# Moving the start address of the weight tiles by 192 bytes within 512

## The chip, the core and the metric

The kernel runs on one core of one Trainium2 chip. The metric is the device time of one execution in microseconds (us). Times of single instructions are in nanoseconds (ns).

## The reference, cut to what matters

The reference runs two networks of two layers each, one after the other, on 256 tokens of 1024 features in float32. The first (below "block 1") has three attention branches and a feed-forward product of width 4096 per layer. The second ("block 2") has gated feed-forward products of width 2816, a retention layer, and a neighbourhood attention. Almost all arithmetic is dense products of this kind:

```python
proj = h @ w_in[layer]
h_res = h_res + merged @ w_out[layer]
h_res = h_res + jnp.square(jax.nn.relu(h2 @ w_ff1[layer])) @ w_ff2[layer]
...
def swiglu(x, w_in, w_out):
    a, b = jnp.split(x @ w_in, 2, axis=-1)
    return (jax.nn.silu(a) * b) @ w_out
```

## The kernel before, in words

Features lie on the 128 partitions, tokens along the free dimension. A float32 product is made of three products of float32r parts: each operand is split into a rounded high part and the rest, and `mm3` (L393 to L397) adds high times high (L395), low weight times high input (L396) and high weight times low input (L397). One such matmul loads a stationary tile of 128 x 128 and streams a moving tile past it. In `mmw` (the dense products) the stationary operand is a chunk of 128 weight columns and the moving operand the activations. In `token_major` (value products of block 2) it is the other way round: activations stand and 256 weight columns move.

`load_w` (L376) fetches a weight block of up to 128 x 1024 into a `raw` tile (ring of four), ScalarE copies it to `whi` (L386, the high part), and VectorE writes the rest to `wlo` (L387). Both `whi` and `wlo` are rings of four tiles of 4096 bytes per partition. All three come from the pool `wp`, in which tags are laid out one after another in the order of first use: `raw`, `whi`, `wlo`. Pools stand behind one another in memory, so that what is added to `wp` moves everything that was opened after it.

The moving operand is 272 columns wide in most of block 1 (256 tokens and 16 others; 256 in parts of it, above all in layer 1), and 512 or 256 in block 2 (two streams of 256 tokens together, or one).

Adding up the tiles' sizes in this order gives the byte address of each tile within a partition. Modulo 512 the program of before has:

```
tile                                              start modulo 512
raw, whi, wlo (every ring buffer, every 128-column chunk)     128
block 1: hh0, hl0, hh1, hl1, ...   64, 128, 192, 256, ... (tiles of 1088 bytes)
block 1, layer 0: uh0, ul0, uh1, ... (moving, 272 wide)   192, 256, 320, ...
block 1, layer 1: uh, ul (moving, 256 wide)                     0
block 2: hh, hl, uh, ul, ra, rb, noh, nol (moving)            320
block 2, retention: ra, rb, pth, ptl (stationary), rvh, rvl (moving)   320
```

A chunk of 128 float32 columns is 512 bytes, so each chunk of a weight tile has the start of its tile. In the retention layer some products take no weights: `scores` multiplies `ra`/`rb` tiles with each other, and `outputs` takes `pth`/`ptl` as stationary and `rvh`/`rvl` as moving operand. Both go through the same `mm3` as the dense products, and in both the two operands start at 320.

The order of the work is the program's order on each engine; the framework puts semaphores between writers and readers. Nothing in this order depends on addresses.

Of the kernel before, what the change touches and what calls it, by code (L numbers as in the profile page):

```python
# [34 lines left out]
# ---------------------------------------------------------------- host layout  # L35
def blocks(w, n):
    """[K, N] -> [N/n, 128, (K/128)*n], contiguous per block and partition."""
    k, m = w.shape
    return np.ascontiguousarray(
        w.reshape(k // P, P, m // n, n).transpose(2, 1, 0, 3)  # L40
    ).reshape(m // n, P, (k // P) * n)


def wide(w):
    """[1024, N] -> [N/256, 2, 128, 4*256]: blocks of 256 columns, in two halves of rows."""
    return np.ascontiguousarray(np.stack([blocks(w[:512], 256), blocks(w[512:], 256)], axis=1))


def cols(v):
    """[n*128] -> [128, n]."""  # L50
    return np.ascontiguousarray(v.reshape(-1, P).T)


def rep(v):
    """vector -> the same vector in each of the 128 partitions."""
    return np.ascontiguousarray(np.broadcast_to(v.reshape(1, -1), (P, v.size)))
# [8 lines left out]
def feat(x):  # L65
    """[tok, 1024] -> [128, 8, tok]."""
    return np.ascontiguousarray(x.T.reshape(KC, P, -1).transpose(1, 0, 2))


# order of a 64-wide rotary head in which partners lie 16 partitions apart  # L70
# [65 lines left out]
def nat_bias(rpb):  # L136
    """[16, 15, 31] -> [16, 128, 2, 256]; outside the windows the fill value."""
    h = rpb.shape[0]
    src = np.concatenate([rpb.reshape(h, 15 * 31), np.full((h, 1), NEG, rpb.dtype)], axis=1)
    q = np.arange(T)  # L140
    r, c = q[:, None] // 64, q[:, None] % 64
    a, cc = q[None, :] // 64, q[None, :] % 64
    start = np.clip(c - 8, 0, 48)
    inside = (cc >= start) & (cc < start + 16)
    idx = np.where(inside, (a - r + 7) * 31 + np.clip(cc - c + 15, 0, 30), 15 * 31)
    b = np.take(src, idx.reshape(-1), axis=1).reshape(h, 2, P, T)
    return np.ascontiguousarray(b.transpose(0, 2, 1, 3)).reshape(h, P, 2 * T)
# [80 lines left out]
# ------------------------------------------------------------------- the chip  # L228
def body(tc, a, off, outs, stop=None):
# [34 lines left out]
    # ---- residual, constants, small vectors  # L264
# [34 lines left out]
    # ---- modulations: silu(c) and silu(c_ctx), in every partition, times the rows of w_mod^T  # L299
# [39 lines left out]
    def decays():  # L339
        # log sigmoid of the decays: min(x, 0) - 2 atanh(e / (2 + e)), e = exp(-|x|)  # L340
        dec = V("dec")
        e, den, s2, po = (tl(mini, [P, 8], f"lg{i}", bufs=1) for i in range(4))
        act.activation(e, dec, AF.Abs)
        act.activation(e, e, AF.Exp, scale=-1.0)
        dve.tensor_scalar(den, e, 2.0, None, op0=ALU.add)
        dve.reciprocal(den, den)
        dve.tensor_tensor(e, e, den, ALU.mult)
        dve.tensor_tensor(s2, e, e, ALU.mult)
        dve.tensor_scalar(po, s2, 1.0 / 17, 1.0 / 15, op0=ALU.mult, op1=ALU.add)
        for d in (13, 11, 9, 7, 5, 3, 1):  # L350
            dve.tensor_tensor(po, po, s2, ALU.mult)
            dve.tensor_scalar(po, po, 1.0 / d, None, op0=ALU.add)
        dve.tensor_tensor(po, po, e, ALU.mult)
        dve.tensor_scalar(lg, dec, 0.0, None, op0=ALU.min)
        dve.scalar_tensor_tensor(lg, po, -2.0, lg, ALU.mult, ALU.add)
        dve.tensor_scalar(nlg, lg, -1.0, None, op0=ALU.mult)
        dve.tensor_scalar(lg256, lg, 256.0, None, op0=ALU.mult)
# [13 lines left out]
    def finish(l, j):  # L371
        """the modulations of layer l up to its part j."""
        while len(todo) > (DEPTH - l) * 72 - 24 * (j + 1):
            step()

    # ---- weights: raw, and its two float32r parts  # L376
    def load_w(src):
        done[0] += 1
        if done[1] and done[0] % done[1] == 0:
            step()  # L380
        n = src.shape[-1]
        raw = tl(wpool, [P, 1024], "raw", bufs=RAW)
        nc.sync.dma_start(raw[:, :n], src)
        hi = tl(wpool, [P, 1024], "whi", F32R, bufs=4)
        lo = tl(wpool, [P, 1024], "wlo", F32R, bufs=4)
        act.activation(hi[:, :n], raw[:, :n], AF.Copy)  # L386
        dve.tensor_tensor(lo[:, :n], raw[:, :n], hi[:, :n].bitcast(F32), ALU.subtract)  # L387
        return hi, lo
# [4 lines left out]
    def mm3(out, w, x, start, stop):  # L393
        """out += w^T x of the parts (hi, lo) of both."""
        pe.matmul(out, w[0], x[0], start=start, stop=False)  # L395
        pe.matmul(out, w[1], x[0], start=False, stop=False)  # L396
        pe.matmul(out, w[0], x[1], start=False, stop=stop)  # L397

    def mmw(out, w, xs, base=0, stride=P, first=True, last=True):
        """out = sum over chunks k of W[:, k]^T x_k, W[:, k] at base + k*stride."""  # L400
        m = len(xs)
        for k, x_ in enumerate(xs):
            o = base + k * stride
            mm3(out, cut(w, slice(o, o + P)), x_, first and k == 0, last and k == m - 1)

    def lead(ws, xs, parts):
        """the first products after a norm, in the order in which its outcome appears."""
# [8 lines left out]
    # ---- dense products in between the steps of the attentions  # L416
    queue, late = [], []

    def fill():
        """the next dense products of the queue, then what waits for the earlier ones."""  # L420
        d = late[:]
        late.clear()
        if queue:
            queue.pop(0)()
        for f in d:
            f()
# [4 lines left out]
    def weave(gens, lag):  # L431
        """runs the generators, a new one every lag rounds, with dense products in between."""
# [14 lines left out]
    def rstd(ss, n, N):  # L447
        """(ss / n + eps) ** -0.5, as float32."""
# [11 lines left out]
    class Sq:  # L460
        """sums of squares over the features, gathered while the residual grows; the last
        chunk comes in parts of the columns."""
# [18 lines left out]
        def end(self, i, *xs):  # L481
            """the last chunks of part i; the very last one meets the others in the product."""
# [26 lines left out]
    # ================================================================ block 1  # L509
    # The products of a norm take x * gain; what they give is scaled by the rstd of the tokens.  # L510
    class Grown:
        """x[:, c0:] times a gain, as parts, and the sums of squares, chunk by chunk."""
# [31 lines left out]
    def block1_layer(l, grown):  # L544
# [23 lines left out]
        def sq2_of(p, N):  # L568
            """the squares, in their two parts."""
# [12 lines left out]
        # ---- latent projections of the first branch  # L582
        def scaled(p, t, r):
            """the products of a norm, scaled by the rstd of the tokens."""
            dve.tensor_tensor(t, p, r, ALU.mult)
            return t
# [21 lines left out]
        def rope(p, N, g, cos, sin, dst):  # L608
            """dst = rotary(p * g), partners 16 partitions apart."""
# [13 lines left out]
        # ---- softmax attention, query-major scores  # L623
# [6 lines left out]
        def qscale(s, om, m, n, scale):  # L630
            """scale * rsqrt of the mean squares of the queries: [128, segs, m] (queries on partitions)."""
# [16 lines left out]
        def probs(S, qsc):  # L648
            """exp(s - max) [128, SW] of the scaled scores, and 1 / sum [128, segs]."""
# [13 lines left out]
        def transposed(e):  # L663
            """[keys, queries]: latent key tiles [128, 384], first keys [16, Q]."""
# [15 lines left out]
        def attend(heads, v):  # L680
            """heads: (out rows, first value column, width, transposed probabilities)."""
# [74 lines left out]
        # ---- dense products that run between the steps of the attentions  # L756
# [28 lines left out]
        # gates and branch projections, merged in the tiles of the first gates  # L785
# [45 lines left out]
        # ---- stick-breaking attention, key-major scores  # L831
# [46 lines left out]
        # ---- differential attention  # L878
# [75 lines left out]
        def close(k, p, c0, dst, grown):  # L954
            """x_k += p, and what the next norm takes of it."""
# [10 lines left out]
        # ---- feed forward  # L966
# [39 lines left out]
    # ================================================================ block 2  # L1006
# [13 lines left out]
    def ada(l, j, sq, vs):  # L1020
        """the modulated norm of the streams vs, in the parts of sq."""
# [14 lines left out]
    def grow(l, j, vs, prod, sq=None):  # L1036
        """x_k += gate * products, with the squares of it; the last two chunks stream by stream."""
# [21 lines left out]
    def ffn(l, s, j, sq, vs, nparts, every=2):  # L1059
        """one gated feed forward over the streams vs."""  # L1060
# [33 lines left out]
    def token_major(w, h, t, p):  # L1094
        """p = tokens t of h times a block of 256 columns, given in two halves of rows."""
# [4 lines left out]
    def retention(sq):  # L1100
# [8 lines left out]
        def decay(hd):  # L1109
            lf, nlb = lg[:, hd:hd + 1], nlg[:, 4 + hd:5 + hd]  # L1110
            # decays between the streams (first half) and within one (second half)
# [58 lines left out]
        def scores(cd, qk):  # L1170
            # scores, key-major, times the decays
# [78 lines left out]
    def nat(sq):  # L1250
# [30 lines left out]
        def unit(h2, qt):  # L1281
            """one pair of heads over one tile of queries."""
# [63 lines left out]
    class Start:  # L1346
        """the sums of squares of the context, and then of the other stream."""
# [57 lines left out]
```

## Time and profile before

| | |
|---|---|
| median of three runs | 2953.26 us (2950.34 to 2953.97) |
| span of the profiled execution, first to last instruction | 2944.5 us, 8.8 us under the median |
| busy: TensorE / weight loads / VectorE / ScalarE / GpSimd | 99% / 87% / 67% / 48% / 8% |
| mean DMA rate | 144 GB/s |

The profiled execution has no time of its own beside its span; the 8.8 us are what the device time has around it, as far as one execution tells.

TensorE is busy from end to end, but a busy share doesn't tell how fast it goes: the ends of matmuls are modelled and overlap the next. The rate is read from the starts of consecutive matmuls. In what follows, the interval is the time from one matmul's start to the next, taken from the first and last start of a stretch and the number of steps between them.

### The profile page before, as it was taken

The numbers are of one execution on the slowest core, as the hardware profiler recorded it, in microseconds if no ns is written. First come the engines' busy times: TensorE is split into PE (matmuls) and PEld (weight loads), VectorE is DVE, ScalarE is ACT, GpSimd is POOL, SyncE is SP. The second block draws the span as 40 slices with busy tenths as digits, with TensorE's granted clock in tenths as the row PEclk, the third lists the DMA queues.
The fourth block names the chain that finished last, engine by engine and source line by source line (L and its number), as shares of the span: only waits on it lengthen the run. The fifth ranks groups of instructions, "written<-read, shape, count | busy, mean of one in ns | idle before, by whom it ended". The sixth has DMA issues, their size and how long they took to land.

```text
span 2944.5 us, 46123 instructions
## 1 busy us (share of the span) xinstructions
PE 2907.9 (99%) x18084; PEld 2556.6 (87%) x18084; DVE 1975.5 (67%) x3370; ACT 1405.4 (48%) x2487; POOL 241.3 (8%) x216
## 2 busy tenths in 40 slices
PE   8999999999999999999999999999999999999998
PEld 8899999989899988888888888888888888877998
DVE  8787876878876665565776767656566565555665
ACT  7767554677665432334433435332343223444554
POOL 2121100212201000001110101000010000100000
PEclk9999999999999999999999999999999999999999
DMA  6344666545467544442343332444334444332464
GB/s 205 115 131 137 193 199 202 163 136 158 147 209 226 177 144 137 142 147 93 122 134 122 109 115 93 143 143 144 128 108 145 137 141 130 102 108 90 157 188 143
DMA packets 122906, 424.46 MB, mean 144 GB/s; under 512 B 13632, under 2 KB 20160, under 8 KB 122560
## 3 DMA queue, kind: packets, MB, share of 16 engines
q1 hardware_dynamic: 121248, 419.50, 45.2%
q8 instruction: 143, 2.34, 0.3%
q10 hardware_dynamic: 1440, 2.00, 0.2%
q14 instruction: 75, 0.61, 0.1%
HBM read 420.40 MB, written 1.05 MB: 143 GB/s over the span
## 4 chain that ended last, share of the span: by engine, by line
PE 92%; DVE 4%; ACT 2%; issue 1%; DMA 0%; POOL 0%; DVEq 0%; ACTq 0%; POOLq 0%
PE acc L395 28%; PE acc L397 28%; PE acc L396 28%; DVE wlo L387 1%; ACT whi L386 1%; PE att L645 1%; PE att L395 1%; PE att L396 1%; PE att L397 1%; PE att L843 1%; PE acc L1317 0%; PE nr L1307 0%; DVE xn L1030 0%; PE att L1287 0%; DVE hl L1032 0%
## 5 line engine op out<-in xcount | busy, mean ns | idle before, releaser
L386 ACT ACTIVATE whi<-raw 128x1024 fp32r<-128x1024 f32 (+2 forms) x650 | 677.8, 1044 | 828.6 <-PE acc L397 774.2
L395 PE MATMUL acc<-hh,whi 128*128 128x512 f32 (+2 forms) x3200 | 1060.6, 332 | 11.6 <-ACT hh L521 6.2
L396 PE MATMUL acc<-hh,wlo 128*128 128x512 f32 (+2 forms) x3200 | 1053.9, 330 | 2.9 <-DVE wlo L387 2.9
L397 PE MATMUL acc<-hl,whi 128*128 128x512 f32 (+2 forms) x3200 | 1053.4, 331 | 0.3 <-DVE hl L1032 0.3
L387 DVE TENSOR_TENSOR wlo<-raw,whi 128x1024 fp32r<-128x1024 f32 (+2 forms) x650 | 789.0, 1215 | 348.2 <-ACT whi L386 314.7
L395 PEld LDWEIGHTS acc<-hh,whi 128*128 128x128 f32 x3200 | 604.8, 189 | 81.7 <-ACT hh L521 6.2
L396 PEld LDWEIGHTS acc<-hh,wlo 128*128 128x128 f32 x3200 | 604.0, 189 | 63.0 <-DVE wlo L387 3.6
L397 PEld LDWEIGHTS acc<-hl,whi 128*128 128x128 f32 x3200 | 601.7, 188 | 61.2 <-DVE hl L1032 0.9
L326 DVE SCALAR_TENSOR_TENSOR dump<-raw,cs 128x1024 bf16<-128x1024 f32 x288 | 354.7, 1231 | 230.2 <-DMA raw<-in_wmod_dram 228.0
L397 PE MATMUL acc<-ul,whi 128*128 128x256 f32 (+2 forms) x1258 | 410.9, 327 | 0.4
L395 PE MATMUL acc<-uh,whi 128*128 128x256 f32 (+2 forms) x1258 | 410.7, 327 | 0.0
L396 PE MATMUL acc<-uh,wlo 128*128 128x256 f32 (+2 forms) x1258 | 409.8, 326 | 0.0
L397 PEld LDWEIGHTS acc<-ul,whi 128*128 128x128 f32 x1258 | 236.4, 188 | 23.0 <-DVE ul L445 1.0
L395 PEld LDWEIGHTS acc<-uh,whi 128*128 128x128 f32 x1258 | 236.9, 188 | 22.3
L396 PEld LDWEIGHTS acc<-uh,wlo 128*128 128x128 f32 x1258 | 236.7, 188 | 22.3
L479 POOL TENSOR_TENSOR sqacc<-sqacc,sq 128x256 f32<-128x256 f32 (+2 forms) x60 | 75.6, 1260 | 1889.0 <-ACT sq L474 1888.6
L456 ACT ACTIVATE sig<-acc 128x512 f32<-128x512 f32 (+1 forms) x88 | 48.1, 546 | 279.8 <-PE acc L397 279.8
L1042 DVE SCALAR_TENSOR_TENSOR x<-acc,gmod,x 128x256 f32<-128x256 f32 x136 | 65.7, 483 | 172.0 <-PE acc L397 171.3
L395 PE MATMUL acc<-whi,hh 128*128 128x256 f32 x384 | 108.0, 281 | 0.2 <-ACT nq L1261 0.2
L397 PE MATMUL acc<-wlo,hh 128*128 128x256 f32 x384 | 107.6, 281 | 0.0
L396 PE MATMUL acc<-whi,hl 128*128 128x256 f32 x384 | 107.3, 279 | 0.0
L1081 DVE TENSOR_TENSOR sig<-acc,sig 128x512 f32<-128x512 f32 (+1 forms) x88 | 54.9, 624 | 59.7 <-PE acc L397 56.8
(319 smaller groups left out, 3523.2 us busy)
## 6 DMA issues: line engine op xcount, KB each, us to landing
raw<-in_fin_dram SPq DMA_DIRECT2D x176, 512.0 KB, 3.7
raw<-in_wmod_dram SPq DMA_DIRECT2D x144, 512.0 KB, 3.6
raw<-in_wf_dram SPq DMA_DIRECT2D x128, 512.0 KB, 4.1
raw<-in_win_dram SPq DMA_DIRECT2D x104, 512.0 KB, 3.7
raw<-in_fout_dram SPq DMA_DIRECT2D x64, 448.0 KB, 3.4
raw<-in_fout_dram SPq DMA_DIRECT2D x32, 512.0 KB, 4.2
raw<-in_rin_dram SPq DMA_DIRECT2D x32, 512.0 KB, 3.5
raw<-in_wbr_dram SPq DMA_DIRECT2D x24, 512.0 KB, 3.6
```

What stands on the lines that cost most here:

```text
L326: dve.scalar_tensor_tensor(dump, raw, 1.0, cs[:, v], ALU.mult, ALU.mult, accum_out=m[:, v, b:b + 1])
L386: act.activation(hi[:, :n], raw[:, :n], AF.Copy)
L387: dve.tensor_tensor(lo[:, :n], raw[:, :n], hi[:, :n].bitcast(F32), ALU.subtract)
L395: pe.matmul(out, w[0], x[0], start=start, stop=False)
L396: pe.matmul(out, w[1], x[0], start=False, stop=False)
L397: pe.matmul(out, w[0], x[1], start=False, stop=stop)
L456: act.activation(dst, src, AF.Exp, scale=-1.0, **k)
L479: eng.tensor_tensor(self.acc[:, :N], self.acc[:, :N], s[:, :N], ALU.add)
L645: pe.matmul(S[:, c:c + n], q[rows, t0 - q0:t0 - q0 + P], k[rows, 0:n], start=False, stop=i == ns - 1)
L843: pe.matmul(Z[:m, c + lo - k0:c + n], sbk[h2][rows, k0:k0 + m], sbq[h2][rows, lo - q0:Q], start=False, stop=k0 == 0)
L1042: dve.scalar_tensor_tensor(d, p[:, i * T:i * T + T], G(l, vs[i], j, k), d, ALU.mult, ALU.add)
L1081: dve.tensor_tensor(g, pb, g, ALU.mult)
```

## The change

Two tiles that nothing reads or writes are added to the pool `wp`: `gap` (48 floats, 192 bytes) before the first `whi` tile, and `gap1` (80 floats, 320 bytes) behind the first use of `wlo`. So `whi` and `wlo` start at 320 instead of 128 modulo 512. `raw` stays where it was. Both gaps together are 512 bytes, so every tile laid out behind the rings moves by 512 and keeps its start modulo 512. The rest of the diff replaces comments and docstrings by empty lines; it is not shown. With the six new lines, L386 and L387 become L392 and L393, and L395 to L397 become L401 to L403.

```diff
+    gap = []
+
     def load_w(src):
...
         raw = tl(wpool, [P, 1024], "raw", bufs=RAW)
         nc.sync.dma_start(raw[:, :n], src)
+        if not gap:
+            gap.append(tl(wpool, [P, 48], "gap"))
         hi = tl(wpool, [P, 1024], "whi", F32R, bufs=4)
         lo = tl(wpool, [P, 1024], "wlo", F32R, bufs=4)
+        if len(gap) == 1:
+            gap.append(tl(wpool, [P, 80], "gap1"))
         act.activation(hi[:, :n], raw[:, :n], AF.Copy)
```

## Rows read from the trace of the kernel before

**Rows 1.** The page: busy time by engine, granted clock in 40 slices, end-setting chain.

```profile
PE 2907.9 (99%) x18084; PEld 2556.6 (87%) x18084; DVE 1975.5 (67%) x3370; ACT 1405.4 (48%) x2487; POOL 241.3 (8%) x216
...
PEclk9999999999999999999999999999999999999999
...
PE 92%; DVE 4%; ACT 2%; issue 1%; DMA 0%; POOL 0%; DVEq 0%; ACTq 0%; POOLq 0%
```

**Rows 2.** TensorE's groups by shape, 1012 to 2945 us: count, busy us, mean ns.

```profile
L395 PE MATMUL acc<-hh,whi 128*128 128x512 f32 x1312 | 519.0, 396 | 0.3 <-DVE sig L1080 0.3
...
L395 PE MATMUL acc<-uh,whi 128*128 128x512 f32 x486 | 192.2, 396 | 0.0
...
L395 PE MATMUL acc<-hh,whi 128*128 128x256 f32 x540 | 151.9, 283 | 4.0 <-ACT hh L1031 2.4 <-DVE sig L1080 1.7
...
L395 PE MATMUL acc<-whi,hh 128*128 128x256 f32 x384 | 108.0, 281 | 0.2 <-ACT nq L1261 0.2
...
L395 PE MATMUL acc<-uh,whi 128*128 128x256 f32 x260 | 73.1, 281 | 0.0
...
L397 PE MATMUL acc<-rb,whi 128*128 128x512 f32 x120 | 47.4, 396 | 0.0
```

**Rows 3.** Timeline, 512-wide dense products: start us, duration us, engine, line.

```profile
1500.21 0.39 PE L395 MATMUL acc<-hh,whi 128*128 128x512 f32 x1
1500.22 0.19 PEld L396 LDWEIGHTS acc<-hh,wlo 128*128 128x128 f32 x1
...
1511.41 0.39 PE L395 MATMUL acc<-hh,whi 128*128 128x512 f32 x1
```

**Rows 4.** Timeline, retention's `outputs`, 512 wide, no weights.

```profile
1443.79 0.39 PE L395 MATMUL att<-rvh,pth 128*128 128x512 f32 x1
...
1444.49 1.05 ACT L386 ACTIVATE whi<-raw 128x1024 fp32r<-128x1024 f32 x1
...
1444.94 0.39 PE L397 MATMUL att<-rvl,pth 128*128 128x512 f32 x1
...
1451.74 0.39 PE L397 MATMUL att<-rvl,pth 128*128 128x512 f32 x1
```

**Rows 5.** Timeline, retention's `scores`, 512 wide, behind a pause of TensorE.

```profile
1431.43 0.40 PE L396 MATMUL att<-ra,rb 128*128 128x512 f32 x1
...
1432.60 0.39 PE L395 MATMUL acc<-hh,whi 128*128 128x512 f32 x1
```

**Rows 6.** Timeline, 256-wide dense products of the last feed-forward.

```profile
2800.81 0.28 PE L395 MATMUL acc<-uh,whi 128*128 128x256 f32 x1
...
2805.91 0.28 PE L395 MATMUL acc<-uh,whi 128*128 128x256 f32 x1
```

**Rows 7.** Timeline, retention's `scores`, 256 wide, no weights.

```profile
1428.27 0.28 PE L396 MATMUL att<-ra,rb 128*128 128x256 f32 x1
...
1429.47 0.28 PE L397 MATMUL att<-rb,ra 128*128 128x256 f32 x1
```

**Rows 8.** Timeline, `token_major` products, weights moving.

```profile
1525.10 0.28 PE L395 MATMUL acc<-whi,hh 128*128 128x256 f32 x1
...
1530.76 0.28 PE L395 MATMUL acc<-whi,hh 128*128 128x256 f32 x1
```

**Rows 9.** Timeline, second feed-forward product of block 1, layer 1.

```profile
949.92 0.28 PE L395 MATMUL acc<-uh,whi 128*128 128x256 f32 x1
...
955.98 0.28 PE L395 MATMUL acc<-uh,whi 128*128 128x256 f32 x1
```

**Rows 10.** Timeline, second feed-forward product of block 1, layer 0, 272 wide.

```profile
479.80 0.29 PE L395 MATMUL acc<-uh,whi 128*128 128x272 f32 x1
...
485.83 0.29 PE L395 MATMUL acc<-uh,whi 128*128 128x272 f32 x1
```

**Rows 11.** TensorE's groups by shape, 0 to 1012 us.

```profile
L395 PE MATMUL acc<-hh,whi 128*128 128x272 f32 x816 | 239.0, 293 | 6.2 <-ACT hh L521 6.2
...
...
L395 PE MATMUL acc<-uh,whi 128*128 128x256 f32 x256 | 72.0, 281 | 0.0
```

## The prediction

> **What bounds the kernel.** I read four views. First the page [rows 1]: TensorE is busy 99% of the span, 92% of the chain that ends last is its matmuls, and the granted clock is full in every slice, so the upper of its two levels (2.4 GHz) holds throughout. TensorE therefore sets the time, and what matters is how fast its stream of matmuls runs, not who waits. Second, its groups by shape, for the counts [rows 2, 11]. Third, the timeline inside long stretches, for the interval between starts. At 2.4 GHz one column per cycle would be 213.3 ns for 512 columns (512/2.4) and 106.7 ns for 256. The 512-wide dense products don't reach this: 48 steps from 1500.21 to 1511.41 us are 11.20 us, 233.3 ns each, 20 ns or 48 cycles over 512 [rows 3]. Beside each running matmul the next stationary tile is loaded, starting within 0.01 us of it [rows 3]. So two reads of SBUF run side by side, and 9% of the stream is something other than columns.
>
> Fourth, I looked for matmuls of the same shape whose two operands stand otherwise modulo 512. Retention's `outputs` is that: 512 wide, the same `mm3`, the same clock, moving at 320 as in the dense products, but the stationary tile at 320 and not at 128. Its first five steps take 1.15 us (230 ns each), and then 30 steps from 1444.94 to 1451.74 us take 6.80 us: 226.7 ns, 32 cycles over 512 [rows 4]. ScalarE writes a `whi` tile in the middle of this without disturbing it. This is where the change would put all weights. At 256 columns the comparison turns round: the dense products (moving 320, stationary 128) step at 113.3 ns (45 steps, 5.10 us) [rows 6], and `scores`, with both at 320, at 120.0 ns (10 steps, 1.20 us) [rows 7]. These are 16 and 32 cycles over 256. So the relative start is worth 16 cycles a matmul, a gain at 512 columns and a loss at 256.
>
> **The change part by part.** The two gap tiles have no instruction: no DMA, no wait, no semaphore. What stands behind the rings moves by 512 bytes and keeps its start modulo 512. What is left is the new start of `whi` and `wlo` against the other operand. I take it that the start modulo 512 of the two operands decides, and price each class by the row with the same pair of starts.
>
> 1. 512-wide dense products, block 2, moving 320, stationary from 128 to 320. Count 3 x (1312 + 486 + 120) = 5754 [rows 2]. From 233.3 to 226.7 ns: 5754 x -6.67 = -38.4 us. Settling costs 5 steps of 230 instead of 226.7 ns, 17 ns each time [rows 4]. Only where the stream is broken must it settle anew; I allow 60 times, an estimate, +1 us. The other bound is that it never settles: the five steps behind a pause take 1.17 us, 234 ns [rows 5], a change of +4 us. I take the settled value, because rows 4 show 30 steps of it against 5 of the other.
> 2. 256-wide dense products, block 2, moving 320, stationary from 128 to 320. Count 3 x (540 + 260) = 2400 [rows 2], and by the code 192 in the neighbourhood layer's last product and 48 in retention's last: 2640. From 113.3 to 120.0 ns: +17.6 us. The other bound is that they stay at 113.3, 0 us. I take 120, the only row with this pair.
> 3. `token_major`, 3 x 384 = 1152 [rows 2], moving from 128 to 320, stationary at 320. Now 5.66 us for 48 steps, 117.9 ns [rows 8]; after it the pair is that of rows 7, 120.0 ns: +2.4 us. Bounds 113.3 and 120: -5.3 to +2.4 us.
> 4. Block 1, layer 1, second feed-forward product: moving 0, stationary from 128 to 320, 3 x 256 = 768 [rows 11]. Now 6.06 us for 51 steps, 118.8 ns [rows 9]. After it the stationary tile stands 320 ahead of the moving one, and in rows 6 it stands 320 ahead modulo 512 too (128 - 320 = -192, which is 320). So I take 113.3 ns: -4.2 us. Bounds 113.3 and 120: -4.2 to +0.9 us.
> 5. The rest of block 1. Moving tiles are 1088 bytes, so from tile to tile the start steps by 64, and over eight tiles every multiple of 64 is met. Shifting the weights by 192 mostly permutes the pairs: 0 us. The largest classes, 272 wide, count 3 x 816 in the first products [rows 11] and by the code 768 in the second of layer 0, together 3216; they take 125.6 ns a step (6.03 us for 48) [rows 10]. The bounds scale rows 6 and 7 by 272/256: 120.4 and 127.5 ns, so 3216 x -5.2 = -16.7 to 3216 x +1.9 = +6.1 us. An average over eight starts stays far from either.
> 6. ScalarE's copy to `whi` and VectorE's difference meet new starts too. ScalarE is busy 48% and VectorE 67% of the span [rows 1], under TensorE's stream. Were each of the 650 weight blocks 0.1 us dearer on both, the 130 us more would still go into idle time; only where TensorE is waiting for a block, 1% of the span, could some show.
>
> The sum is -38.4 + 1 + 17.6 + 2.4 - 4.2 = -21.6 us. It is made against the profiled execution's span of 2944.5 us, which it takes to 2922.9. The 8.8 us between that span and the median of 2953.3 us lie outside the stream and stay, so the forecast is 2931.7 us, 0.7% less. It passes to the end almost in full, since the stream is the chain; where DVE or ACT stands in the chain (6%) no dense product is being cut.
>
> The trace shows a loading weight and a running matmul that cost each other 16 to 48 cycles a step, by their starts [rows 3, 4, 6, 7]. The Trainium skill says otherwise: its page "TensorE: Matmul & The Clock Gate" (Part 2, step by step) gives TensorE two independent read ports, so that loading the next weights takes no bandwidth from the running matmul, and "SBUF — State Buffer" (Who interferes with whom) has it that "PE and ACT never wait on anyone". By that rule the sum would be 0 and the time 2953.3 us; the rows speak against it here.
>
> **The rivals.**
>
> A. *The start does not decide; nothing moves.* The fast 512-wide rows would then owe their 226.7 ns to something else in `outputs`: another PSUM ring (`att`, not `acc`), or both operands being activations. For it: all of rows 4 and 7 come from one layer. Against it: the same layer shows 226.7 at 512 columns and 120.0 at 256, which no general advantage explains, and the PSUM ring is the same in both. Time 2953 us, within 0.2%, which is about what a measurement of this kernel can tell from no change. The rule of the Trainium skill's page "TensorE: Matmul & The Clock Gate" (Part 2), named above, ends here too; no row shows it.
>
> B. *The 512-wide products don't settle; slower.* There is more than one steady step for one pair of starts: rows 5 show 234 ns with the pair that rows 4 show at 226.7. If the dense products of block 2, with their waits for weights at the head of a group, stay in the slow one, the losses of classes 2 to 4 stand alone: 4 + 17.6 + 2.4 - 4.2 = +20 us, 2973 us. It turns from gain to loss where the mean 512-wide step is above 233.3 - (17.6 + 2.4 - 4.2)/5754 = 230.6 ns, so where 59% of the stream is at 233.3. Against it: the five steps at 234 are all there is of it.
>
> C. *The 256-wide products keep their step.* If a steady step of 113.3 ns exists for the new pair too, classes 2 and 3 cost nothing or gain: -38.4 + 1 - 5.3 - 4.2 = -46.9 us, 2906 us. For it: more than one steady step for a pair is possible, as rows 4 and 5 say. Against it: ten equal steps of 120.0 in rows 7.
>
> **How the numbers follow.** The forecast has 0.73, A 0.11, B 0.08, C 0.08. The predicted time is the forecast's, 2931.7 us. Its own range: class 1 down to three quarters of its gain (+10), class 5 between half its lower bound and all of its upper (-8 to +6), class 2 a third less (-6): 2918 to 2947 us. All of it is faster by over 0.2%. With A the cases hold 0.84; so the range reaches from 2918 to A at 2955 and leaves out B and C. Faster 0.73 + 0.08 = 0.81, within 0.2% 0.11, slower 0.08.
>
> **What would show it.** In the profile after, at the same clock: 512-wide dense steps of 226.7 ns and not 233.3 in the feed-forwards of block 2; 256-wide steps of 120.0 and not 113.3 in the last feed-forward, whose 1584 matmuls (by the code, 44 x 24 and 8 x 66) should take 10.6 us more; 113.3 and not 118.8 in layer 1's second product; and about 125.6 in layer 0's. The counts by shape must be unchanged. The prediction is wrong if the 512-wide step stays at 233.3, if the 272-wide step moves by more than 2 ns, or if TensorE waits longer for `whi` or `wlo`.

## The result

The changed kernel takes 2920.69 us (median of four runs, 2918.56 to 2921.71) against 2951.8 us of before in the same comparison (2947.14 to 2953.97): a ratio of 0.990, 95% interval 0.9888 to 0.9912. The span of the profiled execution goes from 2944.5 to 2916.8 us, 27.7 us less. The forecast was 2931.7 us, in a range from 2918 to 2955.

The page of the changed kernel, the lines that answer to [rows 1], and the two groups of `load_w` (busy us, mean ns of one | idle time before them and what ended most of it):

```profile
span 2916.8 us, 46123 instructions
PE 2881.7 (99%) x18084; PEld 2567.2 (88%) x18084; DVE 1974.1 (68%) x3370; ACT 1406.2 (48%) x2487; POOL 241.2 (8%) x216
PEclk9999999999999999999999999999999999999999
PE 94%; DVE 3%; ACT 2%; issue 1%; DMA 1%; POOL 0%; DVEq 0%; SPq 0%; ACTq 0%; POOLq 0%
L392 ACT ACTIVATE whi<-raw 128x1024 fp32r<-128x1024 f32 (+2 forms) x650 | 677.7, 1044 | 812.6 <-PE acc L403 765.0
L393 DVE TENSOR_TENSOR wlo<-raw,whi 128x1024 fp32r<-128x1024 f32 (+2 forms) x650 | 788.7, 1215 | 340.9 <-ACT whi L392 307.2
```

The counts are those of [rows 1], 18084 matmuls and as many weight loads; the granted clock is full in all 40 slices again, so the difference isn't the clock's. ScalarE and VectorE are busy as long as before; most of ScalarE's idle time ahead of its copy still ends with TensorE (765.0 of 812.6 us), and VectorE's ahead of its difference with that copy (307.2 of 340.9). TensorE has the same number of matmuls, done in 26.2 us less of busy time. So the time came out of the stream itself.

TensorE's groups by shape from 1008 us on, beside [rows 2]. The lines of `mm3` have moved from L395 to L397 down to L401 to L403:

```profile
L401 PE MATMUL acc<-hh,whi 128*128 128x512 f32 x1312 | 510.9, 389 | 0.4 <-DVE sig L1086 0.4
...
L401 PE MATMUL acc<-uh,whi 128*128 128x512 f32 x486 | 189.1, 389 | 0.0
...
L401 PE MATMUL acc<-hh,whi 128*128 128x256 f32 x539 | 153.9, 288 | 3.9 <-ACT hh L1037 2.4 <-DVE sig L1086 1.5
```

The mean of one 512-wide matmul falls from 396 to 389 ns, and that of a 256-wide one rises from 283 to 288 ns: both signs of the forecast in one view. These durations overlap, so they tell a direction and no price. The price comes from the starts. The timeline of the changed kernel (start us, duration us), in order: 512-wide dense, 256-wide dense of the last feed-forward, `token_major`, layer 1's second feed-forward product, layer 0's second product:

```profile
1479.85 0.39 PE L401 MATMUL acc<-ra,whi 128*128 128x512 f32 x1
...
1491.41 0.39 PE L401 MATMUL acc<-hh,whi 128*128 128x512 f32 x1
...
2799.77 0.28 PE L401 MATMUL acc<-hh,whi 128*128 128x256 f32 x1
...
2805.89 0.28 PE L401 MATMUL acc<-hh,whi 128*128 128x256 f32 x1
...
1512.84 0.28 PE L401 MATMUL acc<-whi,hh 128*128 128x256 f32 x1
...
1518.96 0.28 PE L401 MATMUL att<-ra,ra 128*128 128x256 f32 x1
...
948.82 0.28 PE L401 MATMUL acc<-uh,whi 128*128 128x256 f32 x1
...
954.94 0.28 PE L401 MATMUL acc<-uh,whi 128*128 128x256 f32 x1
...
480.06 0.29 PE L401 MATMUL acc<-uh,whi 128*128 128x272 f32 x1
...
485.72 0.29 PE L401 MATMUL acc<-uh,whi 128*128 128x272 f32 x1
```

These are 51 steps in 11.56 us (226.7 ns, [rows 3] had 233.3), 51 in 6.12 us (120.0 ns, [rows 6] 113.3), 51 in 6.12 us (120.0 ns, [rows 8] 117.9; the last row is the start of the next product), 54 in 6.12 us (113.3 ns, [rows 9] 118.8), and 45 in 5.66 us (125.8 ns, [rows 10] 125.6). In these stretches every pair of starts steps as forecast.

Summed over the whole trace, from each matmul's start to the next one's, pauses included:

| class | steps | before, us | after, us | difference | forecast |
|---|---|---|---|---|---|
| 1: 512-wide dense, block 2 | 5754 | 1344.9 | 1307.3 | -37.6 | -37.4 |
| 2: 256-wide dense, block 2 | 2628 | 314.2 | 325.4 | +11.2 | +17.6 |
| 3: `token_major` | 1152 | 140.2 | 143.2 | +3.0 | +2.4 |
| 4: layer 1, second feed-forward product | 768 | 91.1 | 87.1 | -4.0 | -4.2 |
| 5: rest of the dense products of block 1 | 5928 | 756.3 | 756.7 | +0.4 | 0 |
| together | | | | -27.0 | -21.6 |

The five classes hold 27.0 of the span's 27.7 us. Class 2 alone is off by more than a microsecond. Of it, the last feed-forward's 1584 matmuls go from 185.6 to 194.2 us, 8.6 more, where 10.6 were forecast.

### The profile page after: what moved, and what is told of

The parts are those of the page before. It is cut to its first block, busy times and chain, and to the rows that moved or that the text cites. A ratio compares the mean times of both kernels' runs of the same rounds, so it can differ in the third digit from the quotient of the medians.

```text
span 2916.8 us, 46123 instructions
## 1 busy us (share of the span) xinstructions
PE 2881.7 (99%) x18084; PEld 2567.2 (88%) x18084; DVE 1974.1 (68%) x3370; ACT 1406.2 (48%) x2487; POOL 241.2 (8%) x216
## 4 chain that ended last, share of the span: by engine, by line
PE 94%; DVE 3%; ACT 2%; issue 1%; DMA 1%; POOL 0%; DVEq 0%; SPq 0%; ACTq 0%; POOLq 0%
PE acc L401 28%; PE acc L403 28%; PE acc L402 28%; PE att L651 1%; DVE wlo L393 1%; ACT whi L392 1%; PE att L401 1%; PE att L402 1%; PE att L403 1%; PE att L849 1%; PE acc L1323 0%; PE nr L1313 0%; PE att L1293 0%; DVE xn L1036 0%; PE att L690 0%
## 5 line engine op out<-in xcount | busy, mean ns | idle before, releaser
L392 ACT ACTIVATE whi<-raw 128x1024 fp32r<-128x1024 f32 (+2 forms) x650 | 677.7, 1044 | 812.6 <-PE acc L403 765.0
L401 PE MATMUL acc<-hh,whi 128*128 128x512 f32 (+2 forms) x3200 | 1055.6, 330 | 11.4 <-ACT hh L527 6.1
L402 PE MATMUL acc<-hh,wlo 128*128 128x512 f32 (+2 forms) x3200 | 1049.0, 328 | 2.5 <-DVE wlo L393 2.5
L403 PE MATMUL acc<-hl,whi 128*128 128x512 f32 (+2 forms) x3200 | 1046.9, 329 | 0.3 <-DVE hl L1038 0.3
L393 DVE TENSOR_TENSOR wlo<-raw,whi 128x1024 fp32r<-128x1024 f32 (+2 forms) x650 | 788.7, 1215 | 340.9 <-ACT whi L392 307.2
L401 PEld LDWEIGHTS acc<-hh,whi 128*128 128x128 f32 x3200 | 605.1, 189 | 73.4 <-ACT hh L527 6.1
L402 PEld LDWEIGHTS acc<-hh,wlo 128*128 128x128 f32 x3200 | 605.1, 189 | 54.6 <-DVE wlo L393 3.3
L403 PEld LDWEIGHTS acc<-hl,whi 128*128 128x128 f32 x3200 | 603.7, 189 | 52.9 <-DVE hl L1038 0.7
L401 PE MATMUL acc<-uh,whi 128*128 128x256 f32 (+2 forms) x1258 | 407.9, 324 | 0.0
L403 PE MATMUL acc<-ul,whi 128*128 128x256 f32 (+2 forms) x1258 | 407.5, 324 | 0.0
L402 PE MATMUL acc<-uh,wlo 128*128 128x256 f32 (+2 forms) x1258 | 406.7, 323 | 0.0
L403 PEld LDWEIGHTS acc<-ul,whi 128*128 128x128 f32 x1258 | 237.3, 189 | 19.5 <-DVE ul L451 0.6
L401 PEld LDWEIGHTS acc<-uh,whi 128*128 128x128 f32 x1258 | 237.2, 189 | 19.3
L402 PEld LDWEIGHTS acc<-uh,wlo 128*128 128x128 f32 x1258 | 237.2, 189 | 19.2
L401 PE MATMUL acc<-whi,hh 128*128 128x256 f32 x384 | 109.4, 285 | 0.2 <-ACT nq L1267 0.2
L403 PE MATMUL acc<-wlo,hh 128*128 128x256 f32 x384 | 109.1, 284 | 0.0
L402 PE MATMUL acc<-whi,hl 128*128 128x256 f32 x384 | 108.9, 284 | 0.0
```

## The experiments

In what follows the *distance* is the start of the stationary tile less that of the moving one, modulo 256 bytes. In block 2's dense products, where the weights are stationary, it is 64 before (128 - 320 = -192) and 0 with the change; in `token_major`, where they move, it is 192 before (320 - 128) and 0 with the change. A *running step* is one under 1.15 times the median of its class; longer ones are pauses. Unless said otherwise an edit is made to the changed kernel, and a ratio is to the kernel before on the same chip, with its 95% interval.

**The layout moved, the starts modulo 512 kept.** One gap of 512 bytes ahead of `whi` and none behind `wlo`:

```diff
-            gap.append(tl(wpool, [P, 48], "gap"))
+            gap.append(tl(wpool, [P, 128], "gap"))
...
-            gap.append(tl(wpool, [P, 80], "gap1"))
+            gap.append(None)
```

> Everything behind the raw tiles is moved by 512 bytes, the weight tiles too, so that they stay at 128 modulo 512. If the start modulo 512 against the other operand decides (the theory): 512-wide dense steps of 233.3 ns, 256-wide ones mostly at 113.3, ratio to before 1.00. If it is the moved layout behind the rings (rival): the ratio of the change, 0.99, and 226.7 ns.

2947.47 us, ratio 0.9993 (0.9983 to 1.0002). All that the change moves is moved, except the start modulo 512, and nothing is gained. The timeline, 512 wide, 48 steps in 11.20 us, is at the 233.3 ns of [rows 3]:

```profile
1500.21 0.40 PE L401 MATMUL acc<-hh,whi 128*128 128x512 f32 x1
...
1511.41 0.39 PE L401 MATMUL acc<-hh,whi 128*128 128x512 f32 x1
```

**The other operand moved instead.** In the kernel before, an unused tile of 320 bytes at the head of block 2's pool `small2` puts the moving tiles of block 2 at 128; the weights stay at 128:

```diff
     small = es2.enter_context(mk("small2", 2))
+    tl(small, [P, 80], "gap2", bufs=1)
```

> The kernel before, its weights at 128, with a gap of 320 bytes in the first pool of block 2, so that the moving tiles there start at 128 instead of 320 modulo 512. Theory (the two starts against each other decide): block 2 as in the change, 226.7 ns at 512 columns and 120.0 at 256; block 1 as before, so without the 4 us of layer 1: ratio 0.991 to 0.993. Rival (the address 320 of the weight tiles is itself better): as before, 233.3 and 113.3 ns, ratio 1.00.

2923.95 us, ratio 0.9914 (0.9897 to 0.9930). The weight pool is untouched, and the 512-wide step falls all the same, 51 steps in 11.56 us, 226.7 ns:

```profile
1479.91 0.39 PE L395 MATMUL acc<-ra,whi 128*128 128x512 f32 x1
...
1491.47 0.39 PE L395 MATMUL acc<-hh,whi 128*128 128x512 f32 x1
```

The 256-wide running step rises to 119.8 ns, as with the change. Layer 1's second product, which this edit doesn't reach, keeps 118.7 ns; without the 4 us that the change gains there this kernel should be slower than the changed one, and it is by 3.3 us (2923.95 against 2920.69), though the two intervals overlap. So it is the relative start of the two operands that acts, not the address of the weights.

**`raw` moved too**, so that ScalarE and VectorE read and write at equal starts again, as before the change:

```diff
     wpool = es.enter_context(mk("wp"))
+    tl(wpool, [P, 48], "gap")
...
-        if not gap:
-            gap.append(tl(wpool, [P, 48], "gap"))
...
-        if len(gap) == 1:
+        if not gap:
             gap.append(tl(wpool, [P, 80], "gap1"))
```

> The change with the first gap ahead of the raw tiles, so that raw, whi and wlo all start at 320. Theory: as the change, ratio 0.99, the same steps. Rival (ScalarE and VectorE read raw and write whi and wlo at other starts against each other, and the weights are ready sooner): the gain goes, ratio 1.00, or the copy to whi and the difference to wlo change from 1044 and 1215 ns.

2918.35 us, ratio 0.9897 (0.9883 to 0.9912), the same as the change, with running steps of 226.8 and 119.8 ns. ScalarE's copy stays at some 1044 ns and VectorE's difference at 1214 to 1215. The rival fell: the split of the weights shows no part in the effect.

**The period.** Weights at 64 instead of 320, which is 256 further round:

```diff
-            gap.append(tl(wpool, [P, 48], "gap"))
+            gap.append(tl(wpool, [P, 112], "gap"))
...
-            gap.append(tl(wpool, [P, 80], "gap1"))
+            gap.append(tl(wpool, [P, 16], "gap1"))
```

> The weight tiles at 64 modulo 512 (gaps of 448 and 64 bytes), which is 256 away from the 320 of the change. If only the distance modulo 256 counts: block 2 as in the change, 226.7 and 120.0 ns, ratio 0.99. If the distance modulo 512 counts: other steps; the ratio can then lie anywhere between 0.98 and 1.02, and the step at 512 columns isn't 226.7 ns.

2918.59 us, ratio 0.990 (0.9886 to 0.9915); running steps 226.8 and 119.8 ns, those of the change. In the timeline, 48 steps in 10.88 us, 226.7 ns:

```profile
1480.14 0.39 PE L401 MATMUL acc<-ra,whi 128*128 128x512 f32 x1
...
1491.02 0.39 PE L401 MATMUL acc<-hh,whi 128*128 128x512 f32 x1
```

Layer 1's second product, at the distance 64 by 64 - 0 where the change has it by 320 - 0, keeps the change's 113.4 ns. What counts repeats every 256 bytes, not every 512 as I had assumed.

**Other distances: weights at 192, then at 256** (distances 128 and 192):

```diff
-            gap.append(tl(wpool, [P, 48], "gap"))
+            gap.append(tl(wpool, [P, 16], "gap"))
...
-            gap.append(tl(wpool, [P, 80], "gap1"))
+            gap.append(tl(wpool, [P, 112], "gap1"))
```

> The weight tiles at 192 modulo 512, 128 away from the moving tiles of block 2. Theory: again other steps, the same in every dense product of a width; the only row with this distance is layer 1's second product before the change, 118.8 ns at 256 columns, so about that in block 2 (+13 us), and at 512 columns a step between 226.7 and 233.3 ns or beyond it: ratio 0.99 to 1.01. Rival (there are two kinds of address only, good and bad): exactly the time of the change or exactly that of before.

```diff
-            gap.append(tl(wpool, [P, 48], "gap"))
+            gap.append(tl(wpool, [P, 32], "gap"))
...
-            gap.append(tl(wpool, [P, 80], "gap1"))
+            gap.append(tl(wpool, [P, 96], "gap1"))
```

> The weight tiles at 256 modulo 512, 64 away from the moving tiles of block 2. Theory: a step of its own again; the nearest row is token_major before the change, 117.9 ns at 256 columns with a few groups at 113.3; at 512 columns no row has it: ratio 0.985 to 1.01. Rival (two kinds of address only): 0.99 or 1.00 exactly.

At 192: 2952.61 us, ratio 1.0011 (1.0001 to 1.0021), 48 steps in 11.16 us (232.5 ns):

```profile
1499.83 0.39 PE L401 MATMUL acc<-hh,whi 128*128 128x512 f32 x1
...
1510.99 0.39 PE L401 MATMUL acc<-hh,whi 128*128 128x512 f32 x1
```

At 256: 2927.37 us, ratio 0.9924 (0.9909 to 0.9939), 48 steps in 10.98 us (228.8 ns):

```profile
1490.24 0.39 PE L401 MATMUL acc<-ra,whi 128*128 128x512 f32 x1
...
1501.22 0.39 PE L401 MATMUL acc<-hh,whi 128*128 128x512 f32 x1
```

The mean running steps at 512 and 256 columns are 232.7 and 119.1 ns at 192, 228.9 and 117.5 ns at 256: steps of their own, as the theory had it. The times alone would not part them from the rival's two kinds: 1.0011 lies next to 1.00, and the interval of the second overlaps that of the change (0.9888 to 0.9912).

The second is a check in three classes at once. Layer 1's second product has the distance 0 there (256 - 0) and goes to 120.0 ns, the step of the last feed-forward in the changed kernel. `token_major` stands at the distance 64 (320 - 256) and mostly steps at 113 ns. Only the 512-wide dense products meet a distance, 192, for which the kernel before has no 512-wide row.

**32 bytes beside the good start: weights at 352 and at 288** (distances 32 and 224):

```diff
-            gap.append(tl(wpool, [P, 48], "gap"))
+            gap.append(tl(wpool, [P, 56], "gap"))
...
-            gap.append(tl(wpool, [P, 80], "gap1"))
+            gap.append(tl(wpool, [P, 72], "gap1"))
```

> The weight tiles at 352, 32 bytes ahead of the moving tiles of block 2, half a step on from 320 towards 384. Theory with steps of 64 bytes as the grain: between the change (226.8 ns at 512 columns, 119.8 at 256) and the distance 64 (233.3 and 114 to 115), ratio 0.988 to 1.00. Rival (only equal starts give the short step): at 512 columns at once 230 ns or more, ratio 0.995 or above.

```diff
-            gap.append(tl(wpool, [P, 48], "gap"))
+            gap.append(tl(wpool, [P, 40], "gap"))
...
-            gap.append(tl(wpool, [P, 80], "gap1"))
+            gap.append(tl(wpool, [P, 88], "gap1"))
```

> The weight tiles at 288, 32 bytes behind the moving tiles of block 2. Theory: between the change (226.8 and 119.8 ns) and the distance 192 of e6 (228.9 and 117.5 ns), ratio 0.988 to 0.993. Rival (only equal starts give the short step): 230 ns or more at 512 columns, ratio 0.995 or above.

At 352: 2955.16 us, ratio 1.0021 (1.0011 to 1.0031). At 288: 2953.61 us, ratio 1.0017 (1.0007 to 1.0027). Both lose all of the gain, and both timelines show 48 steps in 11.20 us, 233.3 ns, the first two rows at 352 and the second two at 288:

```profile
1500.23 0.40 PE L401 MATMUL acc<-ra,whi 128*128 128x512 f32 x1
...
1511.43 0.40 PE L401 MATMUL acc<-hh,whi 128*128 128x512 f32 x1
```

```profile
1500.11 0.40 PE L401 MATMUL acc<-ra,whi 128*128 128x512 f32 x1
...
1511.31 0.40 PE L401 MATMUL acc<-hh,whi 128*128 128x512 f32 x1
```

I had expected a grain of 64 bytes, with a step in between for a start 32 bytes off. The rival held: at the distance 0 the step is 226.7 ns, and 32 bytes either way it is 233.3.

**Only `whi` at 320, `wlo` at 128.** The second gap goes between the rings:

```diff
         hi = tl(wpool, [P, 1024], "whi", F32R, bufs=4)
-        lo = tl(wpool, [P, 1024], "wlo", F32R, bufs=4)
         if len(gap) == 1:
             gap.append(tl(wpool, [P, 80], "gap1"))
+        lo = tl(wpool, [P, 1024], "wlo", F32R, bufs=4)
```

> Only the whi ring at 320, wlo stays at 128 (the second gap stands between the rings). Two of the three matmuls of each product hold whi. If each matmul's own pair of starts prices it: two thirds of the way, 228.9 ns mean at 512 columns and 117.8 at 256, ratio about 0.993. Rival (the stream has to stay at one distance to settle at all): no gain at 512 columns, ratio 1.00 or above.

2941.96 us, ratio 0.9974 (0.9965 to 0.9984). Two of the three matmuls in `mm3` have `whi`. Priced one by one, the 512-wide mean would be 233.3 - 6.6 x 2/3 = 228.9 ns; it is 231.1, a third of the way (in the timeline 48 steps in 11.10 us, 231.3 ns), and the ratio lies between what the theory and the rival gave. At 256 columns the mean is 117.8, the two thirds that were expected.

```profile
1499.71 0.39 PE L401 MATMUL acc<-hh,whi 128*128 128x512 f32 x1
1499.72 0.19 PEld L402 LDWEIGHTS acc<-hh,wlo 128*128 128x128 f32 x1
1499.94 0.40 PE L402 MATMUL acc<-hh,wlo 128*128 128x512 f32 x1
1499.95 0.19 PEld L403 LDWEIGHTS acc<-hl,whi 128*128 128x128 f32 x1
1500.18 0.39 PE L403 MATMUL acc<-hl,whi 128*128 128x512 f32 x1
...
1510.81 0.39 PE L401 MATMUL acc<-hh,whi 128*128 128x512 f32 x1
```

So a matmul's step isn't set by its own pair alone. By line, from each matmul's start to the next one's over the whole trace, the 512-wide running means are 229.1 ns (L401), 235.8 (L402) and 228.4 (L403). The long step is that of the matmul that holds `wlo`, although a `whi` tile is loaded beside it; beside L401 it is `wlo` that is loaded, and that step is short. The 7 ns between the two pairs are still there, but every step is some 2 ns over what its own pair has in a kernel of one distance (226.8, 233.3, 226.8). At 256 columns the three lines are nearly alike (117.6, 118.3 and 117.7 ns). What adds the 2 ns isn't separated by this run.

**Both widths at their better distance.** The change gains at 512 columns and loses at 256. Here the stream of the last feed-forward (and of the last product of the neighbourhood layer) is shifted by 192 bytes on top of the change, so that its 256-wide moving tiles start at 0, and the distance is 64 again:

```diff
         h = htiles()
+        off_ = 48 if len(vs) == 1 else 0
...
+            c = slice(c.start + off_, c.stop + off_)
...
-        return [cut(t, slice(0, T * len(vs))) for t in h]
+        return [cut(t, slice(off_, off_ + T * len(vs))) for t in h]
...
+            if len(vs) == 1:
+                tl(fp, [P, 48], "gapf")
...
+        tl(np_, [P, 48], "gapn")
```

> The change, and in the last feed-forward and the neighbourhood layer's last product, both 256 wide, the moving tiles are placed 192 bytes further, at 0 modulo 512, so that these have the distance that the 256-wide products had before (0 to 320), while the 512-wide ones keep that of the change. Theory: the 1584 + 192 matmuls go from 120.0 back to 113.3 ns, 1776 x -6.67 = -11.8 us against the change if all of them settle there, -9 us at the share that did before: 2909 to 2912 us, ratio 0.986 to 0.987. Rival (the 256-wide step of 120 comes from the weights' own address): the time of the change, ratio 0.990.

2911.87 us (2911.43 to 2912.35), ratio 0.9873 (0.9858 to 0.9888): 0.3% under the changed kernel, whose interval begins where this one ends. But the 1584 matmuls of the last feed-forward take 188.9 us, only 5.3 less than the 194.2 us of the change, half of the 10.6 that 6.7 ns each would give. The timeline tells why, in two stretches of the same product with the same starts:

```profile
2734.78 0.28 PE L401 MATMUL acc<-hh,whi 128*128 128x256 f32 x1
...
2740.91 0.28 PE L401 MATMUL acc<-hh,whi 128*128 128x256 f32 x1
...
2799.88 0.28 PE L401 MATMUL acc<-hh,whi 128*128 128x256 f32 x1
...
2805.88 0.28 PE L401 MATMUL acc<-hh,whi 128*128 128x256 f32 x1
```

54 steps in 6.13 us are 113.5 ns, and 51 in 6.00 us are 117.6 ns. Of the 1584 steps, 514 are at 115 ns or less and 1040 between 115.5 and 119.5. There are two settled steps for one distance, each kept through hundreds of matmuls.

**The same with the moving tiles at 256** (112 floats for the 48, everywhere), the same distance modulo 256 by another address, to see whether the mix goes away:

```diff
-        off_ = 48 if len(vs) == 1 else 0
+        off_ = 112 if len(vs) == 1 else 0
...
-                tl(fp, [P, 48], "gapf")
+                tl(fp, [P, 112], "gapf")
...
-        tl(np_, [P, 48], "gapn")
+        tl(np_, [P, 112], "gapn")
```

> As e8, but the 256-wide moving tiles of the last feed-forward and of the neighbourhood layer's last product at 256 instead of 0 modulo 512; the weights at 320 are then 64 bytes ahead of them, where e8 has them 320 ahead, the same distance modulo 256. In e8 the last feed-forward settled at 113.3 ns in some groups and near 118 in most. If the distance modulo 256 fixes only which two steps there are, and the start of a group picks one: a mix again, 2904 to 2913 us, ratio 0.985 to 0.988. Rival (the distance modulo 512 separates the two steps, as token_major in e6, at 64, was mostly at 113.3): all at 113.3, 1584 x -4.5 = -7 us against e8, about 2905 us.

2910.0 us (2906.27 to 2912.62), ratio 0.9866 (0.9848 to 0.9885). The last feed-forward takes 187.4 us, with 838 steps at 113 ns and 717 near 118: a mix again, in another proportion, and the rival fell. The intervals of these two overlap, so neither is the better; both run under the changed kernel.

## Why the prediction was right, and what it mis-sized

**The premise** held: the relative start of the two operands sets the step of TensorE's stream. Moving the weights without changing it gives nothing, and changing it without moving the weights gives 0.9914. The premise named the starts modulo 512; the runs show that the difference modulo 256 is enough. For the pairs that the prediction priced, both readings give the same step, so no term suffers.

**Class 1** was -38.4 + 1 and came out at -37.6. The mean of the running steps after is 226.8 ns, so what settling costs is 0.1 ns x 5754 = 0.6 us.

**Class 2** is the mis-sized term: forecast +17.6 us, measured +11.2. The step after was right (119.8 ns). The step before was read from 45 matmuls at 113.3 ns [rows 6], and of the class's steps only 2100 of 2628 (80%) are at 113 to 114 there; most others are at 117 to 119, and the mean of the running steps is 114.1. At these means the 2628 steps cost 15.0 us more and not 17.6: one stretch was taken for the class, where a count of all its steps would have given 114.1. The larger part of the miss, 3.8 us, lies in the pauses, which the prediction left out of this class. What they take beyond a running step is 14.2 us before, in 97 pauses, and 10.5 after, in 79. That a slower stream waits less is one reading of this and not shown: the kernel with the layout moved, at 115.1 ns a step, has 76 pauses and 11.6 us.

**Classes 3 and 4** came out at +3.0 and -4.0 for +2.4 and -4.2. For class 4 the only support was a row at the same distance in another product, and it held: 113.3 ns.

**Class 5**: 756.3 to 756.7 us. Starts that run through all multiples of 64 keep their average, 125.5 to 125.7 ns at 272 columns.

**Class 6**: ScalarE's and VectorE's instructions didn't change, so the cover I named for them wasn't needed.

**From span to median.** The sum on the span was 2922.9 us, and the span is 2916.8: 6.1 us, of which class 2 is 6.4. The rest of the miss against the median, 2931.7 - 2920.69 = 11.0 us, is that I carried over 8.8 us as time outside the stream. In the changed kernel the profiled execution has a span of 2916.8 us and a time of 2918.56: 1.8 us lie around it, and in every other run on record whose span is known 1.7 to 1.9. The rest of the 8.8 us is the place of one execution among the others (2947.14 to 2953.97 us before), and a single span near the lower end of that scatter can't be extended by it. The median after is 3.9 us above its span.

**The rivals.** A, that the start doesn't decide, fell with the first two experiments. The rule behind it is the Trainium skill's ("TensorE: Matmul & The Clock Gate", Part 2: loading the next weights takes nothing from the running matmul). By that rule the start would change nothing; in the runs it changes a 512-wide step by 6.7 ns, 226.7 against 233.3, with nothing but one operand's start moved. B fell: of class 1's 5754 steps after the change 5623 take 225 to 228 ns. C fell for this change, as the 256-wide steps went to 120.0. Its reason was sound, though: more than one steady step for a pair exists. It is seen at the distance 64 and not at 0, and it cost class 2 the 2.6 us of its step before.

**What stays open.** The prediction laid the cost on the load that runs beside a matmul. That these two reads collide in SBUF or on the way from it is argued from their overlap in [rows 3], and not shown. The run with `whi` alone at 320 speaks against its simplest form: as the trace records the starts, the step is long where the matmul's own tile is `wlo` (235.8 ns), and not where `wlo` is the tile being loaded (229.1 ns). Nor is it shown what picks 113.3 or 118 ns at the distance 64. Layer 1's second product in the changed kernel has 763 of 768 steps at 113 or 114 ns at this distance, the last feed-forward of the last two experiments a mix, so the distance alone doesn't decide it. Nor do the starts modulo 512: with the layout moved by 512 they are those of before, and 363 steps of the last feed-forward lie between 115.5 and 119.5 ns where before has 13.

## What to carry to other kernels

Where TensorE is busy from end to end, measure the step from start to start in long stretches, for each pair of shapes; a busy share of 99% hid 3% of the 512-wide step here. If products of one shape step differently, compare the starts of their stationary and moving tiles: two unused tiles of 512 bytes together were worth 1% here. The sign turned with the width, so each width gets its own distance. Price a class by all its steps, not by one clean stretch of it.

## What the runs showed of the hardware that was not expected

Mean running steps of `mm3` in float32r parts at the full clock, by the distance of the starts modulo 256 bytes:

| distance | runs (weights at, moving at) | 512 columns, ns | 256 columns, ns |
|---|---|---|---|
| 0 | the change (320, 320); 128, 128; 64, 320 | 226.8 | 119.8 |
| 32 | 352, 320 | 233.3 | 118.3 |
| 64 | before (128, 320); moved by 512 | 233.3 | 114.1 to 115.1 |
| 64 | last feed-forward of the last two experiments (320, 0; 320, 256) | none | 115.4 to 116.3 |
| 128 | 192, 320 | 232.7 | 119.1 |
| 192 | 256, 320 | 228.9 | 117.5 |
| 224 | 288, 320 | 233.3 | 116.9 |

- The best distance for 512 columns is the worst for 256. No distance that was run is good for both.
- Which operand the weights are makes no difference that these runs show. `token_major`, whose weights move, has nearly the same 256-wide steps by distance: 119.9 ns at 0, 118.3 at 32, 114.3 at 64, 118.9 at 128, 117.1 to 117.8 at 192 and 116.7 at 224.
- The effect has a grain of 32 bytes or less and a period of 256, narrower and shorter than I had looked for.
- At one distance, 64, there are two settled steps at 256 columns, 113.3 and some 118 ns, that persist through hundreds of matmuls.
- With only two of three matmuls at the good distance, a third of the gain at 512 columns comes and not two thirds (231.1 ns).
